# Cutting the last stage of a block kernel into pieces of 512, 384 and 128 tokens in place of 512, 256 and 256

## The chip, the core and the metric

The kernel runs on one core of a Trainium2 chip. The metric is the device time of one execution in microseconds; a comparison goes by the median of several runs.

## The reference

One layer of a streaming encoder, with 1024 tokens, 1024 channels (`D`) and a hidden width of 2816 (`DFF`): a mixing sub-layer, a gated feed-forward sub-layer, and a last root-mean-square norm. Only the end matters here:

```python
        a, bgate = jnp.split(jnp.einsum('bsd,df->bsf', h2, w_ffn_in[l]), 2, axis=-1)
        x = x + g2 * jnp.einsum('bsf,fd->bsd', jax.nn.silu(a) * bgate, w_ffn_out[l])

    return rms_norm(x, final_norm_g)
```

The final norm divides each token by the root of its mean square over all 1024 channels and multiplies each channel by a gain. So no output of a token can be scaled before all of its channels are there.

## The kernel before

Activations lie transposed: channels on the 128 partitions, tokens along the free axis. `x1[j]` for j from 0 to 7 is the residual of channel chunk j, 128 x 1024 in f32. Matrix products keep f32 precision by splitting every operand into a high and a low part in `fp32r`; one product of chunks is then three matmuls, high by high, high by low and low by high (`mm3`, L348, L349, L351), each with its own 128x128 weight load. Sums over partitions are matmuls with a matrix of ones in plain f32 (L1354), for which the profile shows two matmul rows each.

The feed-forward output product sums over 22 row chunks of the hidden tensor (`FC`). Eighteen of them are done by a scheme with seven products per 2x2 block in three groups; their results are added onto `x1`. The last four (`REST` = 18 to 21) are done plainly, and this is the stage that the change touches. Its tokens are cut into pieces (`PIECES`, L115), and the final norm of one piece is laid beside the products of the next:

- `piece_out(i, j)` (L1305): 12 matmuls for output chunk j of piece i into a PSUM tile `y`; VectorE evicts it by scaling it with the gate and adding `x1` (L1314); ScalarE squares the result (L1317). Where `on_pool(i, j)` is true, ScalarE then multiplies the chunk by its gain in place (L1321), since GpSimd is to do a plain product later.
- `piece_sum(i, j)` (L1324): VectorE adds the squares of chunk j to the sum.
- `piece_norm(i, parts)` (L1349): TensorE sums over partitions (`ss`); ScalarE takes the reciprocal root (L399, called through `rstd_start`) and half of its square (`rq`, L1356).
- `piece_rstd` (L1359): VectorE refines the root by one Newton step, `rft` (L1363) and `rf` (L1365). For the last piece `rf` lies in PSUM, for others in SBUF.
- `piece_scale(i, rf)` (L1328): chunk after chunk, GpSimd (L1342, by `rf` or for the last piece by an SBUF copy of it, `rp`, L1333) or VectorE (L1344, by gain and `rf` at once) scales, and SyncE issues the output DMA (L1347). With pieces narrower than 512 tokens, m = 512 / n chunks go into one tile and one DMA.

The loop at L1368 runs over pieces and, within one, over j. From the second piece on, after chunk 1 (`NORM_AT`) it emits the sum of the piece before, and after chunk 3 that piece's root and scales. For the last piece the root and the scales come behind everything, with the sum over four parts, the running sum of chunks 0 to 4 and the single squares of 5, 6 and 7 (`APART`). All chunks of the first two pieces are scaled on GpSimd, and of the last piece chunks 0, 3 and 5 (`POOL_LAST`), the others on VectorE.

Each engine works through its instructions in order, as the program emits them with `issue_after` hints; so do the DMA queues, among them SyncE's, which issues all outputs.

Of the kernel before, what the change touches and what calls it, by code (L numbers as in the profile page):

```python
# [38 lines left out]
ALU = mybir.AluOpType  # L39
# [5 lines left out]
KC = D // P  # L45
# [55 lines left out]
NORM_AT = 1  # L101
LAG = 2
APART = 3
POOL_LAST = (0, 3, 5)


PRODUCTS = "1265734"
# [4 lines left out]
REST = 2 * GROUP * GROUPS  # L112


PIECES = [(0, 512), (512, 256), (768, 256)]  # L115


FILL = 248
# [3 lines left out]
def block_kernel(ctx: ExitStack, tc: tile.TileContext, x0, xT, c, vecs, ada, w_first, w_plain, w_duals,  # L122
                 w_short, w_conf, w_o, w_fi, w_fo, w_last, outT):
    nc = tc.nc
# [27 lines left out]
    def ps_tile(name):  # L152
        return psp.tile([P, H], F32, tag="ps", name=name)

    def ps2_tile(name):
        return ps2p.tile([P, H], F32, tag="ps2", name=name)
# [1112 lines left out]
    n = 2 * GROUP * P  # L1269
# [26 lines left out]

    LAST = len(PIECES) - 1

    def wide_tile(name):
        return hl_tile(name, dt=F32)  # L1300

    def on_pool(i, j):
        return i < LAST or j in POOL_LAST

    def piece_out(i, j):  # L1305
        at, n = PIECES[i]
        h, off = at // H, at % H
        o = ps_tile("y")[:, :n]
        for f in range(REST, FC):
            xs = tuple(t[:, off : off + n] for t in hid[f, h])  # L1310
            c0 = (j % 4) * P
            mm3([o], slice(c0, c0 + P), ws[f, j // 4], [xs], f == REST, f == FC - 1)
        dst = x1[j][:, at : at + n]
        evac = nc.vector.scalar_tensor_tensor(out=dst, in0=o, scalar=modc(40 + j), in1=dst, op0=ALU.mult, op1=ALU.add)  # L1314
        piece_out.ins = evac.ins
        sq = wide_tile("sq")[:, :n]
        act = nc.scalar.activation(sq, dst, AF.Square, scale=1.0 / 32.0)  # L1317
        if i == LAST and j == KC - 1:
            load_rsqrt(act.ins)
        if on_pool(i, j):  # L1320
            nc.scalar.activation(dst, dst, AF.Copy, scale=ng[:, V_GFIN + j : V_GFIN + j + 1])  # L1321
        sqs.append(sq)

    def piece_sum(i, j):  # L1324
        with tc.issue_after(piece_out.ins):
            nc.vector.tensor_tensor(sqs[0], sqs[0], sqs[j], ALU.add)

    def piece_scale(i, rf):  # L1328
        at, n = PIECES[i]
        m = H // n  # L1330
        if i == LAST:
            rp = wide_tile("rp")[:, :n]
            nc.scalar.copy(rp, rf)  # L1333
        else:
            rp = rf
        for j in range(0, KC, m):
            ys = wide_tile("y") if m > 1 else x1[j][:, at : at + n]
            ys = ys.rearrange("p (m n) -> p m n", n=n)
            for d in range(m):
                y, src = ys[:, d], x1[j + d][:, at : at + n]  # L1340
                if on_pool(i, j + d):
                    nc.gpsimd.tensor_tensor(y, src, rp, ALU.mult)  # L1342
                else:
                    nc.vector.scalar_tensor_tensor(  # L1344
                        out=y, in0=src, scalar=ng[:, V_GFIN + j + d : V_GFIN + j + d + 1], in1=rf, op0=ALU.mult, op1=ALU.mult
                    )
            nc.sync.dma_start(outT[j : j + m, :, at : at + n].rearrange("m p n -> p m n"), ys)  # L1347

    def piece_norm(i, parts):  # L1349

        n = PIECES[i][1]
        ss, r, q = (t[:, :n] for t in (ps_tile("ss"), wide_tile("rf"), wide_tile("rq")))
        for part in parts:
            nc.tensor.matmul(ss, ones, part, start=part is parts[0], stop=part is parts[-1])  # L1354
        rstd_start(ss, eps1, "rf", n, lambda name: r)
        nc.scalar.activation(q, r, AF.Square, scale=0.5 ** 0.5)  # L1356
        return ss, r, q

    def piece_rstd(i, ss, r, q):  # L1359

        n = PIECES[i][1]
        t = ps2_tile("rft")[:, :n]
        nc.vector.scalar_tensor_tensor(out=t, in0=ss, scalar=EPS, in1=q, op0=ALU.add, op1=ALU.mult)  # L1363
        out = ps2_tile("rf")[:, :n] if i == LAST else r
        nc.vector.scalar_tensor_tensor(out=out, in0=t, scalar=1.5, in1=r, op0=ALU.subtract, op1=ALU.mult)  # L1365
        return out

    for i in range(len(PIECES)):  # L1368
        acc, sqs = sqs[0] if i else None, []
        lag = LAG if i == LAST else 0  # L1370
        for j in range(KC):
            piece_out(i, j)
            if j > lag and j - lag < KC - APART * (i == LAST):
                piece_sum(i, j - lag)
            if i and j == NORM_AT:
                norm = piece_norm(i - 1, [acc])
            if i and j == NORM_AT + 2:
                with tc.issue_after(piece_out.ins):
                    rf = piece_rstd(i - 1, *norm)
                piece_scale(i - 1, rf)  # L1380
    piece_scale(LAST, piece_rstd(LAST, *piece_norm(LAST, [sqs[0]] + sqs[KC - APART :])))


# [70 lines left out]
```

## Time and profile before

| | us |
|---|---|
| median of 3 runs | 1476.24 |
| their range | 1476.24 to 1478.43 |
| the profiled execution | 1477.93 |
| span of its instructions | 1476.2 |
| first piece, 512 tokens, from the first matmul | 1419.6 to 1441.2 |
| middle piece, 256 tokens | 1441.2 to 1453.6 |
| last piece, 256 tokens | 1453.6 to 1465.7 |
| from there to the end of the span | 10.5 |

PE is TensorE's matmuls, PEld its weight loads, DVE VectorE, ACT ScalarE, POOL GpSimd, SP SyncE. A row of a timeline gives the start from the beginning of the span, the duration (both in us), the engine, the line of the kernel, the operation, what it writes and reads, the shape and how many instructions are merged into the row; in brackets stands the idle time of the engine before it and what ended that. A row of a group gives count, busy time, mean duration in ns, and idle time before. Matmuls are pipelined: a matmul's duration includes its way through the array, and the pace is read from the distance of starts.

### The profile page before, as it was taken

Reading aid. Unit: us, or ns where it says so; the run is one execution under the profiler, and the core shown is the slowest. Engines: PE = TensorE matmul, PEld = TensorE weight load, DVE = VectorE, ACT = ScalarE, POOL = GpSimd, SP = SyncE. Lnnn points to the kernel's source line nnn. Section 1 sums busy time; section 2 is a strip of 40 time slices with the busy share of each in tenths; the row PEclk is TensorE's granted clock in tenths of the full one; section 3 lists DMA queues with packets and bytes.
Section 4 is the critical chain, followed back from the end, with each engine's and each line's share of the span. In section 5 each row is a group of like instructions: output and inputs, shape, how many; then the busy total and the mean of one; then the engine's idle time right before and its main releaser. Section 6 shows DMA issues by size and latency. Waiting matters only on the chain.

```text
span 1476.2 us, 17809 instructions
## 1 busy us (share of the span) xinstructions
PE 1462.0 (99%) x6475; PEld 1200.4 (81%) x6475; DVE 1177.7 (80%) x1623; ACT 617.0 (42%) x896; POOL 513.3 (35%) x459
## 2 busy tenths in 40 slices
PE   9999999999999999999999999999999999999997
PEld 5888888888888888878888878888888888888887
DVE  7999888887998969999687699777777765677755
ACT  4653433333333335555235465444444443222235
POOL 0036677767877771111022001101111015535005
PEclk9999999999999999999999999999999999999999
DMA  8522213222222267376685337655455449988403
GB/s 342 188 64 72 100 58 128 72 86 100 91 67 86 82 219 285 105 237 213 200 311 172 117 100 235 209 176 168 150 192 166 146 149 371 357 287 276 156 1 115
DMA packets 83274, 245.36 MB, mean 166 GB/s; under 512 B 9585, under 2 KB 11761, under 8 KB 83186
## 3 DMA queue, kind: packets, MB, share of 16 engines
q1 hardware_dynamic: 42352, 136.01, 27.6%
q0 software_dynamic: 36944, 95.44, 19.6%
q10 hardware_dynamic: 3890, 12.78, 2.3%
q8 instruction: 51, 0.84, 0.2%
q14 instruction: 37, 0.30, 0.1%
HBM read 181.79 MB, written 62.39 MB: 165 GB/s over the span
## 4 chain that ended last, share of the span: by engine, by line
PE 91%; DVE 6%; DMA 1%; issue 1%; ACT 1%; POOL 0%; POOLq 0%; DVEq 0%; ACTq 0%
PE bank L351 11%; PE bank L348 11%; PE bank L349 11%; PE x L351 7%; PE x L348 7%; PE x L349 7%; PE z L349 4%; PE z L348 4%; PE z L351 4%; PE y L349 3%; PE y L348 3%; PE y L351 3%; PE yb L351 2%; PE yb L348 2%; PE yb L349 2%; PE mix L349 2%
## 5 line engine op out<-in xcount | busy, mean ns | idle before, releaser
L220 ACT CAST wh<-raw 128x1024 fp32r<-128x1024 f32 (+2 forms) x254 | 256.3, 1011 | 485.2 <-PE bank L349 133.6
L221 POOL TENSOR_TENSOR wl<-raw,wh 128x1024 fp32r<-128x1024 f32 x84 | 204.5, 2444 | 81.8 <-ACT wh L220 81.8
L221 DVE TENSOR_TENSOR wl<-raw,wh 128x1024 fp32r<-128x1024 f32 (+2 forms) x170 | 195.0, 1147 | 47.5 <-ACT wh L220 46.2
L838 DVE SCALAR_TENSOR_TENSOR c<-diff,vec,c 128x512 f32<-128x512 f32 x232 | 171.0, 753 | 4.4
L1170 POOL DMA_DIRECT2D hid<-stage x71 | 37.8, 533 | 347.0 <-DVE stage L389 341.0
L348 PE MATMUL bank<-th,wh 128*128 128x512 f32 x288 | 112.0, 389 | 0.0
L349 PE MATMUL bank<-tl,wh 128*128 128x512 f32 x288 | 112.0, 389 | 0.0
L351 PE MATMUL bank<-th,wl 128*128 128x512 f32 x288 | 112.0, 389 | 0.0
L838 DVE SCALAR_TENSOR_TENSOR c<-u,wsum,c 128x512 f32<-128x512 f32 x112 | 84.3, 753 | 2.6
L240 POOL TENSOR_TENSOR raw<-raw 128x1024 f32<-128x1024 f32 x12 | 29.2, 2430 | 130.4 <-DVE wl L221 92.8
L388 ACT CAST stage<-g 128x512 fp32r<-128x512 f32 x62 | 38.4, 622 | 65.9 <-DMA hid<-stage 35.4
L351 PEld LDWEIGHTS bank<-th,wl 128*128 128x128 f32 x288 | 54.1, 188 | 11.3
L349 PEld LDWEIGHTS bank<-tl,wh 128*128 128x128 f32 x288 | 54.1, 188 | 11.2
L348 PEld LDWEIGHTS bank<-th,wh 128*128 128x128 f32 x288 | 54.1, 188 | 11.2
L389 DVE TENSOR_TENSOR stage<-g,stage 128x512 fp32r<-128x512 f32 x62 | 42.4, 689 | 25.3 <-ACT stage L388 25.3
L1196 POOL DMA_DIRECT2D th<-hid x71 | 38.0, 535 | 53.2 <-PE x L351 31.9
L348 PE MATMUL x<-th,wh 128*128 128x512 f32 x144 | 56.1, 390 | 0.0
L349 PE MATMUL x<-tl,wh 128*128 128x512 f32 x144 | 56.0, 389 | 0.0
L351 PE MATMUL x<-th,wl 128*128 128x512 f32 x144 | 56.0, 389 | 0.0
L348 PE MATMUL yb<-zsh,wh 128*128 128x512 f32 x128 | 49.8, 389 | 0.0
L349 PE MATMUL yb<-zsl,wh 128*128 128x512 f32 x128 | 49.8, 389 | 0.0
L351 PE MATMUL yb<-zsh,wl 128*128 128x512 f32 x128 | 49.8, 389 | 0.0
(798 smaller groups left out, 4211.3 us busy)
## 6 DMA issues: line engine op xcount, KB each, us to landing
hid<-stage POOLq DMA_DIRECT2D x71, 512.0 KB, 4.4
raw<-in_w_fi SPq DMA_DIRECT2D x51, 512.0 KB, 3.7
raw<-in_w_duals SPq DMA_DIRECT2D x48, 512.0 KB, 3.5
th<-hid POOLq DMA_DIRECT2D x71, 256.0 KB, 5.7
tl<-hid POOLq DMA_DIRECT2D x71, 256.0 KB, 5.7
ada<-in_ada SPq DMA_DIRECT2D x24, 512.0 KB, 5.9
raw<-in_ada SPq DMA_DIRECT2D x24, 512.0 KB, 4.6
raw<-in_w_fo SPq DMA_DIRECT2D x24, 384.0 KB, 5.7
```

The source lines that it names most:

```text
L220: hi = nc.scalar.copy(wh, raw)
L221: lo = lo_engine.tensor_tensor(wl, raw, f32(wh), ALU.subtract)
L240: eng.tensor_tensor(a["s1"], a["21"], a["22"], ALU.add)
L348: nc.tensor.matmul(ps, wh, xh, start=first, stop=False, skip_group_check=again)
L349: nc.tensor.matmul(ps, wh, xl, start=False, stop=False, skip_group_check=again)
L351: mm3.ins = nc.tensor.matmul(ps, wl, xh, start=False, stop=last, skip_group_check=again).ins
L388: t_split.act = nc.scalar.copy(hi, src).ins
L389: t_split.ins = nc.vector.tensor_tensor(lo, src, f32(hi), ALU.subtract).ins
L838: tap.ins = nc.vector.scalar_tensor_tensor(out=out, in0=src[:, s : s + H], scalar=wt, in1=acc, op0=ALU.mult, op1=ALU.add).ins
L1170: nc.gpsimd.dma_start(hid_dram[key], s)
L1196: nc.gpsimd.dma_start(t, hid_dram[key][:, s])
```

## The change

`PIECES` becomes 512, 384 and 128 tokens. `POOL_SCALES` tells for each piece which chunks GpSimd scales: all of the first, 0 to 4 of the middle one, and 0, 3 and 5 of the last as before. Chunks 5, 6 and 7 of the middle piece are scaled by VectorE, and they are emitted after the last chunk of the last piece, ahead of the last piece's own sum, root and scales; their output DMAs are issued there. ScalarE no longer multiplies these three chunks by their gain. The middle piece's root now lies in PSUM, so ScalarE makes an SBUF copy of it for GpSimd. With m = 512 // 384 = 1 the middle piece is scaled in place and has eight output DMAs of one chunk; the last has two DMAs of four chunks each (4 x 128 tokens).

In each engine's order the count of TensorE's instructions stays the same; VectorE gets four more, ScalarE two fewer and GpSimd three fewer, and SyncE issues 18 output DMAs in place of 16.

```diff
-POOL_LAST = (0, 3, 5)
+POOL_SCALES = (range(KC), range(5), (0, 3, 5))
...
-PIECES = [(0, 512), (512, 256), (768, 256)]
+PIECES = [(0, 512), (512, 384), (896, 128)]
...
     def on_pool(i, j):
-        return i < LAST or j in POOL_LAST
+        return j in POOL_SCALES[i]
...
-    def piece_scale(i, rf):
+    def piece_scale(i, rf, chunks=range(KC), rp=None):
+
         at, n = PIECES[i]
         m = H // n
-        if i == LAST:
+        if i and rp is None:
             rp = wide_tile("rp")[:, :n]
             nc.scalar.copy(rp, rf)
-        else:
-            rp = rf
-        for j in range(0, KC, m):
+        for j in chunks[::m]:
             ys = wide_tile("y") if m > 1 else x1[j][:, at : at + n]
...
                 if on_pool(i, j + d):
-                    nc.gpsimd.tensor_tensor(y, src, rp, ALU.mult)
+                    nc.gpsimd.tensor_tensor(y, src, rp if i else rf, ALU.mult)
...
-        out = ps2_tile("rf")[:, :n] if i == LAST else r
+        out = ps2_tile("rf")[:, :n] if i else r
...
-                piece_scale(i - 1, rf)
+                piece_scale(i - 1, rf, range(KC)[: len(POOL_SCALES[i - 1])])
+    with tc.issue_after(piece_out.ins):
+        piece_scale(LAST - 1, rf, range(len(POOL_SCALES[LAST - 1]), KC), ())
     piece_scale(LAST, piece_rstd(LAST, *piece_norm(LAST, [sqs[0]] + sqs[KC - APART :])))
```

## The prediction

> **What bounds the kernel now.** I read the page first (shares, then the chain), then the windows by stage, then each engine's timeline over the last 40 us.
>
> ```profile
> span 1476.2 us, 17809 instructions
> PE 1462.0 (99%) x6475; PEld 1200.4 (81%) x6475; DVE 1177.7 (80%) x1623; ACT 617.0 (42%) x896; POOL 513.3 (35%) x459
> 1419.60:1441.20 21.60, 21.60 (x97) 17.87 (x96) 10.16 (x14) 9.49 (x14) 0.00 (x0) 1.00 0.00 1
> 1441.20:1453.60 12.40, 12.40 (x100) 11.91 (x99) 8.66 (x16) 8.86 (x17) 3.02 (x3) 1.00 0.06 23
> 1453.60:1465.70 12.10, 12.10 (x101) 11.92 (x100) 8.42 (x17) 6.92 (x16) 10.84 (x10) 1.00 0.44 169
> 1465.70:1476.20 10.50, 1.88 (x10) 1.23 (x8) 3.40 (x8) 1.77 (x5) 5.12 (x8) 0.85 0.52 182
> ```
>
> The last four rows are the windows: length, then busy time of PE, PEld, DVE, ACT, POOL, granted clock, DMA share and GB/s. They are the three pieces and the tail. In the pieces PE is busy all the time at clock 1.00, so any extra TensorE time there moves the end. In the tail (10.5 us) TensorE only does the last sum, and a chain of small steps sets the end. The change touches both: it re-cuts the two later pieces and shortens the steps of the tail.
>
> **TensorE, the dear part.** Each piece is 8 output blocks of 12 products (4 row chunks of `hid`, 3 products each), 96 in all, whatever its width. Their pace is read from starts:
>
> ```profile
> 1424.88 0.39 PE L348 MATMUL y<-th,lwh 128*128 128x512 f32 x1
> 1441.20 0.28 PE L348 MATMUL y<-th,lwh 128*128 128x256 f32 x1
> 1443.96 0.28 PE L351 MATMUL y<-th,lwl 128*128 128x256 f32 x1
> 1456.32 0.28 PE L351 MATMUL y<-th,lwl 128*128 128x256 f32 x1
> 1456.53 0.30 PEld L1354 LDWEIGHTS ss<-sq,ones 128*128 128x128 f32 x2
> 1456.85 0.19 PEld L348 LDWEIGHTS y<-th,lwh 128*128 128x128 f32 x1
> 15.25 2.31 PEld L535 LDWEIGHTS clock<-rx0r,ones 128*128 128x128 f32 x20
> 1465.57 0.28 PE L351 MATMUL y<-th,lwl 128*128 128x256 f32 x1
> 1465.69 1.89 PE L1354 MATMUL ss<-sq,ones 128*128 128x256 f32 x8
> ```
>
> From 1424.88 to 1441.20 lie 72 products of 512 columns: 0.227 us each. From 1441.20 to 1443.96 lie 23 steps of 256: 0.120 us each. The straight line through both is 0.013 us plus 0.107 us per 256 columns; it gives 0.173 us for 384 columns and 0.067 us for 128.
>
> At 128 columns the line need not hold, because every product loads its own 128x128 weights. Two rows tell what a load takes. At 1456.53 TensorE is idle (the product before started at 1456.32 and was due for a successor at 1456.44): two loads span 0.30 us there and one lasts 0.19, so the second starts 0.11 us after the first, with nothing else in its way. In the 20 clock-keeping products of 128 columns at 15.25, loads follow each other every (2.31 - 0.19) / 19 = 0.112 us. No row shows loads of this size closer together than that. So I bound a 128-column product from below by 0.112 us, loads back to back. The upper end, while it stays one pass, is 0.123: plain products of 256 columns (the last row: four sums, two rows each, eight rows in 1.89 us, so 0.215 apart) have a fixed part of only 0.002 us over their streaming of 2 x 0.107, these products one of 0.013, and the 0.011 between them may come on top of the load. I take 0.120, the 256-column row, as the nearest: same instruction, same weights. Then the narrow piece costs as much as a 256-column one though it does half the work.
>
> Sum on TensorE: the middle piece goes from 96 x 0.120 to 96 x 0.173, +5.1 us; the last stays at 96 x 0.120, 0.0; the sum over squares of the middle piece is 384 wide in place of 256, 2 x 0.107 = +0.2. The last product of the kernel, at 1465.57 now, starts at T = 1470.9. That is the cost.
>
> **The tail, the gain.** The rows of the tail, with groups that give the slope by width:
>
> ```profile
> 1465.89 0.48 DVE L1314 SCALAR_TENSOR_TENSOR x<-y,mod,x 128x256 f32<-128x256 f32 x1 [0.48 <-PE y L351]
> 1466.41 0.42 ACT L1317 ACTIVATE sq<-x 128x256 f32<-128x256 f32 x1 [1.02 <-DVE x L1314]
> 1467.61 0.47 ACT L399 ACTIVATE rf<-ss,eps 128x256 f32<-128x256 f32 x1 [0.70 <-PE ss L1354]
> 1468.12 0.42 ACT L1356 ACTIVATE rq<-rf 128x256 f32<-128x256 f32 x1
> 1468.57 0.43 DVE L1363 SCALAR_TENSOR_TENSOR rft<-ss,rq 128x256 f32<-128x256 f32 x1 [2.20 <-ACT rq L1356]
> 1469.04 0.43 DVE L1365 SCALAR_TENSOR_TENSOR rf<-rft,rf 128x256 f32<-128x256 f32 x1
> 1469.50 0.37 ACT L1333 COPY rp<-rf 128x256 f32<-128x256 f32 x1 [0.97 <-DVE rf L1365]
> 1469.91 2.05 DVE L1344 SCALAR_TENSOR_TENSOR y<-x,ng,rf 128x256 f32<-128x256 f32 x5 [0.44 <-ACT rp L1333]
> 1469.95 2.09 POOL L1342 TENSOR_TENSOR y<-x,rp 128x256 f32<-128x256 f32 x3 [1.22 <-ACT rp L1333]
> L1314 DVE SCALAR_TENSOR_TENSOR x<-y,mod,x 128x256 f32<-128x256 f32 x16 | 7.6, 480 | 5.8 <-PE y L351 5.7
> L1314 DVE SCALAR_TENSOR_TENSOR x<-y,mod,x 128x512 f32<-128x512 f32 x7 | 5.3, 751 | 5.4 <-PE y L351 5.4
> L1317 ACT ACTIVATE sq<-x 128x256 f32<-128x256 f32 x16 | 6.6, 414 | 8.0 <-DVE x L1314 8.0
> L1317 ACT ACTIVATE sq<-x 128x512 f32<-128x512 f32 x7 | 4.4, 633 | 9.3 <-DVE x L1314 9.3
> ```
>
> DVE loses (751 - 480) / 2 = 0.135 us per 128 columns, ACT 0.11. Counted from T (now 1465.57), with the hand-over of 0.03 to 0.04 us that stands between the rows: eviction T+0.32 to 0.67 (0.345 long), square to 1.02, the two passes of the last summand at 0.112 in place of 0.215 (0.58 in place of 0.78 from the square's end to the next step), reciprocal root 1.60 to 1.96, its square to 2.31, then two DVE steps of 0.30 to 2.98, the copy `rp` to 3.27. Now that copy ends at T+4.30. Five DVE scales of 0.41 - 0.135 take 1.4, to T+4.7; three on POOL about 1.2 (below). Now both end at T+6.47. Gain so far: 1.8 us.
>
> What DVE is given in addition lies in there: three scales of 384 columns, 0.41 + 0.135 = 0.55 each, 1.65 us, are queued between the last eviction (T+0.67) and the first root step (needed at T+2.34). They fill the 2.20 us for which DVE now waits there, shrunk to 1.67. Cost nothing; if DVE is slower beside POOL, each 0.1 us per scale costs 0.3 us at the end, since the whole root chain and the five last scales are queued behind.
>
> Now POOL and SP's queue, past which the three scales are moved.
>
> ```profile
> 1450.58 10.79 POOL L1342 TENSOR_TENSOR x<-x,rf 128x512 f32<-128x512 f32 x8 [81.86 <-DVE rf L1365]
> 1462.63 6.10 POOL L1342 TENSOR_TENSOR y<-x,rf 128x256 f32<-128x256 f32 x8 [1.26 <-DVE rf L1365]
> 1460.13 0.48 DVE L1314 SCALAR_TENSOR_TENSOR x<-y,mod,x 128x256 f32<-128x256 f32 x1 [0.95 <-PE y L351]
> 1462.03 0.42 DVE L1365 SCALAR_TENSOR_TENSOR rf<-rft,rf 128x256 f32<-128x256 f32 x1
> 1464.27 8.73 SPq L1347 DMA_DIRECT2D outT<-y  x8
> 1470.70 2.30 SPq L1347 DMA_DIRECT2D outT<-y  x4
> GB/s 380 357 53 0 0 0 0 0 0 275 374 380 386 340 386 374 386 363 386 380 386 375 380 386 369 65 0 0 0 0 0 0 0 0 0 0 0 0 0 0
> ```
>
> POOL: 10.79 / 8 = 1.35 us for 512 columns, 6.10 / 8 = 0.76 for 256, so 1.06 for 384 and about 0.45 for 128. The root of the first piece waits for four blocks of the middle one, which are 4 x 12 x 0.053 = 2.6 us later, and for wider DVE steps between (0.3), so POOL starts at 1453.4 and ends the first piece at 1464.2 (now 1461.4). The middle piece's products start at 1441.2 as now and end at 1458.7 (96 x 0.173, and two rows of 512 plain columns for the first piece's sum, 2 x 0.43). Its root comes after four blocks of the last piece and its own sum: 1458.7 + 48 x 0.120 + 0.65 = 1465.1. From the fourth block's eviction to the end of `rf` the two DVE rows above stand 2.3 us apart, from start to end; with the hand-over 2.4, and 0.5 for `rp`: POOL starts its five scales at 1468.0 and ends at 1473.3. Its last three can start at T+3.3 = 1474.2: it is free by 0.9 us. Had it kept all eight, it would come 2.3 us late; that is what the move saves.
>
> DMA: the GB/s row covers 1470 to 1477 in slices of 0.175 us. The last piece's 1.05 MB flow at some 380 GB/s from 1471.6 (0.9 us after the issue at 1470.70) to 1474.5, and the span ends 1.7 us later. After, two chains reach for the end. By TensorE: the second half of the last piece is issued at T+4.7, flows from T+5.6 for 0.7 us, and the span ends at T+8.0 = 1478.9. By POOL and SP: the outputs of middle chunks 5 to 7 stand in SP's queue behind chunk 4, which POOL ends at 1473.3. From 1474.2 four chunks of 0.197 MB flow in 2.1 us, to 1476.3, and the last piece's 0.52 MB behind them in 1.4, to 1477.7; the span ends at 1479.4. The second is later. It holds 48 narrow products where the first holds 96: its end is 1473.65 + 48 c for c us per narrow product.
>
> **The sum.** 1479.4 is +3.2 us on the span: +5.3 on TensorE, and a tail of 8.5 us in place of 10.6. The profiled execution took 1477.93 us for its span of 1476.2, so 1.7 lie around it; the median of the runs is 1476.24, and put on that the forecast is 1479.4 us as well. With c = 0.112 it is +2.8, with 0.123 +3.4.
>
> **Rivals.** *The narrow products run on the line, 0.067 us: no change.* Then TensorE ends when it does now, T = 1465.8. For it: nothing but the line. Against it: the two load rows. The tail's gain would still not show, because POOL's chain ends last: 1473.65 + 48 x 0.067 = 1476.9, +0.6 us. The forecast's sign turns on this price: below c = 0.116 the end is within 3.0 us of now. The Trainium skill, "TensorE: Matmul & The Clock Gate", section "Back-to-back issue gap", gives about 81 ns for a sustained pair of weight load and 128-column matmul; by it, an estimate, the end would be 1473.65 + 48 x 0.081 = 1477.5, and this rival would hold. No row of this trace has loads that close.
>
> *The narrow products lose the single pass.* Plain 128-column products come every 0.112 us, and a plain sum needs two of them (eight rows for four sums above): 0.224 us per product, T later by 96 x 0.104 = 10.0 us, TensorE's chain the last: T+8.0 = 1488.9, slower by 0.9%. For it: no row shows this kind of product under 256 columns. Against it: the changed program's instruction order has one product where there was one, of the same kind.
>
> *DVE falls behind.* Sums of squares slow down beside POOL, which now runs through the whole last piece:
>
> ```profile
> 1445.24 0.43 DVE L1326 TENSOR_TENSOR sq<-sq 128x256 f32<-128x256 f32 x1 [0.48 <-ACT sq L1317]
> 1451.30 2.29 DVE L1326 TENSOR_TENSOR sq<-sq 128x256 f32<-128x256 f32 x2
> ```
>
> That is 1.15 us each for the two, against 0.43 before POOL starts. A block of the narrow piece has 1.44 us, eviction and sum then need 1.5: some tenths on top, for the last three scales of the middle piece too (end 1473.2 by the sum, 0.1 before POOL's), within the forecast's range.
>
> **How the numbers follow.** A measurement of this kernel tells about 0.2%, 3.0 us, from no change. The forecast's case (weight loads set the pace) gets 0.70; its own range is +2.0 to +4.5, so it lies on both sides of the bound: 0.42 slower by over 0.2%, 0.28 within. The line gets 0.12 (0.10 within, 0.02 faster, if tail steps are shorter than interpolated). The lost pass gets 0.18, all slower. Together slower 0.60, same 0.38, faster 0.02. The range takes in the first two cases, 1476.0 to 1482.0, and leaves out the third.
>
> **What would show it.** Right: narrow products about 0.12 us apart, the last one starting near 1471, about 8.5 us from there to the end, POOL idle just before its last three scales, DMA without a gap from chunk 4 on. Wrong: a pace near 0.07 (then POOL is busy without a gap to the end) or near 0.22; a root step on DVE that waits for the three scales and not for ACT.

## The result and the profile after

The changed kernel takes 1491.55 us (median of five, 1490.66 to 1492.97) against 1477.35 (1476.24 to 1480.24) for the kernel before on the same chip: slower, ratio 1.0094 with a 95% interval of 1.0081 to 1.0107, +14.2 us where +3.2 was forecast. The profiled execution took 1491.55 us with a span of 1489.7.

TensorE at the start of the stage, in the profile before and then after:

```profile
1419.44 0.39 PE L348 MATMUL y<-th,lwh 128*128 128x512 f32 x1
```

```profile
1422.11 0.39 PE L348 MATMUL y<-th,lwh 128*128 128x512 f32 x1
```

The stage begins 2.7 us later though all that precedes it is the same program. In the first 25 us the granted clock averaged 1.00 in the one profile and 0.93 in the other, but that average does not settle it: in the profiles of other runs below that have 0.93 there too, the stage begins anywhere from 1417.6 to 1423.5. Why the start shifts is not shown; executions of the kernel before scatter by some 4 us. So stages are compared from this row on: from here to the end of the span it is 56.7 us before and 67.6 after, +10.9.

The windows of the changed kernel (length, busy time of PE, PEld, DVE, ACT and POOL, granted clock, DMA share, GB/s):

```profile
1443.90:1461.40 17.50, 17.50 (x99) 17.02 (x98) 10.68 (x16) 10.28 (x17) 5.50 (x4) 1.00 0.12 43
1461.50:1467.90 6.40, 4.55 (x38) 4.14 (x36) 4.39 (x5) 2.07 (x7) 5.64 (x5) 1.00 0.43 166
1468.10:1480.80 12.70, 12.70 (x62) 12.70 (x61) 4.47 (x11) 3.01 (x9) 4.94 (x5) 0.50 0.27 97
1480.80:1489.70 8.90, 2.20 (x10) 1.91 (x9) 3.90 (x11) 1.34 (x5) 1.28 (x3) 0.50 0.37 125
```

The first row is the middle piece, 17.5 us as forecast. The second and third are the last piece: first 1.85 us in which TensorE is not busy, then 12.7 us at a granted clock of 0.50, to the end of the products. TensorE's timeline gives both, and the pace:

```profile
1463.71 0.27 PE L348 MATMUL y<-th,lwh 128*128 128x128 f32 x1
1463.82 0.28 PE L349 MATMUL y<-tl,lwh 128*128 128x128 f32 x1
1463.94 0.28 PE L351 MATMUL y<-th,lwl 128*128 128x128 f32 x1
1466.06 0.91 PE L1353 MATMUL ss<-sq,ones 128*128 128x384 f32 x2 [1.85 <-DVE sq L1326]
...
1480.35 0.41 PE L348 MATMUL y<-th,lwh 128*128 128x128 f32 x1
1480.56 0.41 PE L349 MATMUL y<-tl,lwh 128*128 128x128 f32 x1
1480.78 0.41 PE L351 MATMUL y<-th,lwl 128*128 128x128 f32 x1
```

Narrow products come every 0.11 us at first and every 0.21 at the end. Between them TensorE waits 1.85 us for VectorE's last sum of squares (L1326) before it can sum over partitions. Why that sum is late, VectorE's and GpSimd's timelines show:

```profile
1455.07 0.68 DVE L1364 SCALAR_TENSOR_TENSOR rf<-rft,rf 128x512 f32<-128x512 f32 x1
...
1460.35 0.61 DVE L1314 SCALAR_TENSOR_TENSOR x<-y,mod,x 128x384 f32<-128x384 f32 x1
1461.55 1.68 DVE L1326 TENSOR_TENSOR sq<-sq 128x384 f32<-128x384 f32 x1 [0.59 <-ACT sq L1317]
1463.15 0.61 DVE L1314 SCALAR_TENSOR_TENSOR x<-y,mod,x 128x384 f32<-128x384 f32 x1
1464.35 1.66 DVE L1326 TENSOR_TENSOR sq<-sq 128x384 f32<-128x384 f32 x1 [0.59 <-ACT sq L1317]
```

```profile
1455.90 11.24 POOL L1341 TENSOR_TENSOR x<-x,rf 128x512 f32<-128x512 f32 x8 [85.08 <-DVE rf L1364]
1473.20 4.94 POOL L1341 TENSOR_TENSOR x<-x,rp 128x384 f32<-128x384 f32 x5 [6.07 <-ACT rp L1334]
1484.79 1.28 POOL L1341 TENSOR_TENSOR y<-x,rp 128x128 f32<-128x128 f32 x3 [6.65 <-ACT rp L1334]
```

While GpSimd scales the first piece, from 1455.9 to 1467.1, a sum of 384 columns takes 1.7 us. Eviction, the wait for the square and the sum then take 2.8 us per block (1460.35 to 1463.15), where TensorE gives a block every 2.08 (12 x 0.173). VectorE falls behind by 0.7 us a block over the last blocks of the middle piece.

So two things were seen that the forecast's sum does not contain: a wait of TensorE and a fall of the granted clock. The experiments ask where the wait comes from, and whether the clock falls by the wait, by the thin products, or by both. Products are called thin here when they stream for about half of the time that their weight load takes.

### The profile page after: what moved, and what is told of

The parts are those of the page before. It is cut to its first block, busy times and chain, and to the rows that moved or that the text cites. A ratio compares the mean times of both kernels' runs of the same rounds, so it can differ in the third digit from the quotient of the medians.

```text
span 1489.7 us, 17805 instructions
## 1 busy us (share of the span) xinstructions
PE 1475.6 (99%) x6475; PEld 1212.6 (81%) x6475; DVE 1180.3 (79%) x1626; ACT 617.0 (41%) x894; POOL 512.4 (34%) x456
## 4 chain that ended last, share of the span: by engine, by line
PE 90%; DVE 7%; issue 1%; ACT 1%; DMA 1%; DVEq 0%; ACTq 0%
PE bank L351 11%; PE bank L349 11%; PE bank L348 11%; PE x L351 7%; PE x L349 7%; PE x L348 7%; PE z L348 4%; PE z L351 4%; PE z L349 4%; PE y L351 3%; PE y L349 3%; PE y L348 3%; PE yb L349 2%; PE yb L351 2%; PE yb L348 2%; PE mix L348 2%
## 5 line engine op out<-in xcount | busy, mean ns | idle before, releaser
L351 PEld LDWEIGHTS bank<-th,wl 128*128 128x128 f32 x288 | 54.1, 188 | 11.2
L349 PEld LDWEIGHTS bank<-tl,wh 128*128 128x128 f32 x288 | 54.1, 188 | 11.2
```

The lines of the kernel that those rows point to most:

```text
L349: nc.tensor.matmul(ps, wh, xl, start=False, stop=False, skip_group_check=again)
L351: mm3.ins = nc.tensor.matmul(ps, wl, xh, start=False, stop=last, skip_group_check=again).ins
```

## Experiments

**The sum and the root two blocks later** (the changed kernel otherwise): TensorE has other products to do before it needs VectorE's sum.

```diff
-            if i and j == NORM_AT:
+            if i and j == NORM_AT + 2 * (i == LAST):
...
-            if i and j == NORM_AT + 2:
+            if i and j == NORM_AT + 2 + 2 * (i == LAST):
```

> The changed kernel with the middle piece's sum over partitions and root emitted two blocks later in the last piece, so that TensorE need not wait 1.9 us for VectorE's sums. Two theories on why the granted clock falls to 0.5 some 6.6 us into the narrow piece. Thin products (each 128-column product streams for about 0.053 of the 0.111 us that its weight load takes, and that alone lets the clock down): no wait of TensorE, but the clock falls to 0.5 all the same and the pace goes from 0.111 to 0.213; about 1.9 us under the changed kernel, near 1489.5. Wait (the idle 1.9 us let the clock down): clock 1.00 and 0.111 us to the last product; 1.9 + 7 us under the changed kernel, near 1482.5.

Measured 1482.67 us (seven, 1481.24 to 1484.79; before: 1477.67), ratio 1.0035 (1.0023 to 1.0046). Its window over the whole last piece and its last products:

```profile
1461.10:1472.30 11.20, 11.20 (x99) 10.94 (x97) 7.90 (x16) 4.85 (x15) 5.88 (x6) 1.00 0.31 121
```

```profile
1472.16 0.28 PE L349 MATMUL y<-tl,lwh 128*128 128x128 f32 x1
1472.27 0.28 PE L351 MATMUL y<-th,lwl 128*128 128x128 f32 x1
```

No wait, clock 1.00, 0.11 us to the last product. Thin products alone do not let the clock down; the theory of the wait gave the time within 0.2 us. That closeness is partly luck: from the start of the stage the last product comes 8.2 us earlier than in the changed kernel (50.5 in place of 58.7 us), but the rest takes 10.7 us in place of 8.9, for GpSimd starts its scales of the middle piece only at 1472.1 and its last three directly behind them.

**Twice the work per weight load**: the last piece's products over 256 columns, of which 128 are used.

```diff
+        more = (256 - n) * (i == LAST)
-        o = ps_tile("y")[:, :n]
+        o = ps_tile("y")[:, : n + more]
...
-            xs = tuple(t[:, off : off + n] for t in hid[f, h])
+            xs = tuple(t[:, off - more : off + n] for t in hid[f, h])
...
-        evac = nc.vector.scalar_tensor_tensor(out=dst, in0=o, ...)
+        evac = nc.vector.scalar_tensor_tensor(out=dst, in0=o[:, more:], ...)
```

> The changed kernel with the last piece's products over 256 columns (768 to 1023), of which only the last 128 are evicted and used: twice the streaming per weight load, everything else the same, the 1.9 us wait of TensorE included. Thin products: clock stays at 1.00, pace 0.120; 72 products after the wait at 0.120 in place of 0.213, about 7 us under the changed kernel, near 1484.5 although TensorE does more. Wait: the clock falls to 0.5 as before and 256 columns then take 0.23 us: 1 to 2 us over the changed kernel, near 1493.

Measured 1483.52 us (seven, 1481.72 to 1485.04), ratio 1.0036 (1.0023 to 1.0049):

```profile
1463.61 0.59 PE L1354 MATMUL ss<-sq,ones 128*128 128x384 f32 x1 [1.64 <-DVE sq L1327]
```

```profile
1459.00:1472.90 13.90, 12.26 (x99) 11.80 (x97) 8.47 (x16) 5.20 (x15) 8.94 (x9) 1.00 0.31 118
```

The wait is there, 1.64 us, and the clock stays at 1.00. With twice the products' work the kernel is some 8 us faster than the changed one. This went as the theory of thin products said, the run above as the other. Neither is enough: this fall takes the wait and what surrounds it. The wait is 0.2 us shorter here than in the changed kernel; that this is not the reason, the stretches of the clock show below.

**The kernel before, with a wait put in**: VectorE instructions that leave the values as they are, ahead of the middle piece's last sum; three, two and one of them.

```diff
     def piece_sum(i, j):
+        for _ in range(HOLD * (i == 1 and j == KC - 1)):
+            nc.vector.scalar_tensor_tensor(out=sqs[j], in0=sqs[j], scalar=1.0, in1=sqs[j], op0=ALU.mult, op1=ALU.max)
```

> The kernel before, with three VectorE instructions (sq times 1, maximum with itself: the values stay) put ahead of the middle piece's last sum of squares, so that TensorE waits about 2.3 us at the same place, ahead of the middle piece's sum over partitions. Thin products: clock 1.00 to the end of the products, about +2.3 us, near 1479.5. Wait: the clock falls to 0.5 a few us later, some 60 products of 256 columns at 0.23 us in place of 0.12: +9 us, near 1486.

> The kernel before with two VectorE instructions (values stay) ahead of the middle piece's last sum: a wait of TensorE of about 2.5 to 3 us among 256-column products, longer than the 1.85 us of the changed kernel and shorter than the 4.1 us that halved the clock with three. If the wait's length alone decides, anything over about 1.8 us halves the clock for some 6.8 us: about +2.7 for the wait and +3.3 for the clock, near 1484. If thin products have their part in it, 256-column products around such a wait keep the clock at 1.00: near 1480.5.

> The kernel before with one VectorE instruction (values stay) in place of three put ahead of the middle piece's last sum, for a wait of TensorE of about 1.5 to 2 us among 256-column products. If a wait of that length lets the clock down by itself: clock 0.5 for one or two stretches of 3.41 us, 1.6 to 3.4 us on top of the wait, near 1482. If it takes thin products as well: clock 1.00, the wait alone, near 1479.3.

Measured 1483.65 us with three (ratio 1.0043, 1.0030 to 1.0057), 1482.35 with two (1.0031, 1.0022 to 1.0041), 1478.47 with one (1.0006, 0.9997 to 1.0015). TensorE's waits, in that order, came out at 4.13 us in place of 2.3, at 2.73 and at 1.33, since these instructions, too, took longer beside GpSimd:

```profile
1463.26 0.80 PE L1356 MATMUL ss<-sq,ones 128*128 128x256 f32 x1 [4.13 <-DVE sq L1328]
```

```profile
1457.50 0.48 PE L1356 MATMUL ss<-sq,ones 128*128 128x256 f32 x1 [2.73 <-DVE sq L1328]
```

```profile
1456.12 0.48 PE L1356 MATMUL ss<-sq,ones 128*128 128x256 f32 x1 [1.33 <-DVE sq L1328]
```

The windows with three, and with two:

```profile
1456.20:1461.10 4.90, 2.93 (x25) 2.73 (x23) 3.89 (x7) 2.79 (x6) 4.90 (x4) 1.00 0.44 169
1461.20:1467.90 6.70, 4.64 (x19) 4.46 (x20) 2.85 (x4) 1.60 (x4) 3.13 (x3) 0.50 0.37 145
1468.10:1474.50 6.40, 6.40 (x56) 6.40 (x55) 4.55 (x10) 2.69 (x6) 3.72 (x5) 1.00 0.13 43
```

```profile
1451.80:1458.20 6.40, 3.67 (x29) 3.42 (x29) 5.04 (x8) 3.11 (x7) 6.40 (x5) 1.00 0.46 175
1458.30:1461.60 3.30, 3.30 (x18) 3.30 (x17) 0.48 (x1) 1.24 (x3) 1.52 (x2) 0.50 0.53 205
1461.70:1468.10 6.40, 6.40 (x55) 6.40 (x55) 4.55 (x10) 2.69 (x6) 3.71 (x5) 1.00 0.12 42
```

Among 256-column products a wait of 2.73 or 4.13 us halves the clock too, but it comes back soon: after some 3.4 us with two, some 6.8 with three. That is read from one profile each; the mean clocks of the other executions with two, 0.996 to 0.999, leave open whether it fell in all of them. With three neither theory had the time (1479.5 and 1486). With one, 1.33 us, the clock stays at 1.00 over the whole piece. So thin products are not needed for the fall; a longer wait does it without them. What differs in the changed kernel is that the clock does not come back.

**Wide products late**: the changed kernel with its wait, and blocks 5, 6 and 7 of the last piece over 256 columns as above (`more` only for j > 4).

> The changed kernel, with 1.85 us of wait among thin products as it is, but with the products of blocks 5, 6 and 7 of the last piece over 256 columns (the last 128 used). Theory: thin products, once the clock is halved, keep it there, since they stream for half the time only; wide ones let it recover, as in the kernel with the 4.1 us wait, some 3.4 to 6.8 us after they begin. Then the clock falls near 7 us into the last piece as in the changed kernel and is back at 1.00 before the last product or at it, and the time is 0 to 2.5 us under the changed kernel, near 1490. Rival: once halved this late, the clock stays for 13 us or more whatever the products are: clock 0.5 to the end, and 36 products of 256 columns at 0.213 as before: no change, near 1491.5.

Measured 1488.18 us (four, 1487.15 to 1491.77; before: 1477.33), ratio 1.0074 (1.0055 to 1.0093). The windows, and the first wide products:

```profile
1462.80:1468.10 5.30, 3.46 (x28) 3.14 (x27) 4.39 (x5) 1.00 (x4) 5.30 (x5) 1.00 0.46 176
1468.20:1478.30 10.10, 10.10 (x49) 10.10 (x48) 2.75 (x7) 3.22 (x9) 2.94 (x4) 0.50 0.15 57
1478.50:1481.20 2.70, 2.70 (x25) 2.70 (x25) 1.88 (x4) 1.03 (x3) 2.14 (x3) 1.00 0.61 217
```

```profile
1475.77 0.52 PE L348 MATMUL y<-th,lwh 128*128 128x256 f32 x1
...
1478.43 0.28 PE L348 MATMUL y<-th,lwh 128*128 128x256 f32 x1
```

That is 10.9 us over the kernel before, where the changed kernel has 14.2: some 3 us less, and 0 to 2.5 were expected. The clock stays halved through all the thin products, 7.6 us, and is back 2.6 us after the first wide one. Thin products keep a halved clock down; that is shown. At half clock 256 columns take 0.21 us (1475.77 to 1478.43 hold 12 or 13 products), just as 128 do.

**Only the pieces, without VectorE's share**: the changed kernel with all eight chunks of the middle piece on GpSimd.

```diff
-POOL_SCALES = (range(KC), range(5), (0, 3, 5))
+POOL_SCALES = (range(KC), range(KC), (0, 3, 5))
```

> The changed kernel with all eight chunks of the middle piece left to GpSimd, as the kernel before has it; the pieces stay 512, 384 and 128. GpSimd was idle for 6.6 us ahead of its last three scales, so three more of 1.0 us should fit: within 0.5 us of the changed kernel by either theory on the clock, near 1491.5. If the move of three scales to VectorE had a cost of its own (1.65 us ahead of the root's two steps), this would be faster by up to 1.6 us.

Measured 1490.43 us (four, 1486.39 to 1491.27), ratio 1.0080 (1.0059 to 1.0100), not told apart from the changed kernel. One execution of the four took 1486.39 us with a mean granted clock of 0.997, the others 1490.08 to 1491.27 with 0.991 to 0.992; the one at 1486.39 us is the profiled one, and it has the same wait of 1.85 us. So with one and the same wait the clock need not fall; by the mean clocks it fell in the other three, and about 4 to 5 us hang on it here. Where it holds, GpSimd's eight scales set the end: its last three start at 1479.6, directly behind them, and from the last product to the end are 9.9 us.

**Only VectorE's share, without the pieces**: 512, 256 and 256, with chunks 6 and 7 of the middle one on VectorE at the end.

```diff
-PIECES = [(0, 512), (512, 384), (896, 128)]
+PIECES = [(0, 512), (512, 256), (768, 256)]
...
-POOL_SCALES = (range(KC), range(5), (0, 3, 5))
+POOL_SCALES = (range(KC), range(6), (0, 3, 5))
```

> One part of the change alone: pieces of 512, 256 and 256 as in the kernel before, but VectorE scales the middle piece's chunks 6 and 7 at the end (two in place of three, since two chunks share a DMA), and the middle root is copied for GpSimd. Two scales of 0.41 us fit into the 2.2 us in which VectorE waits for the last root: no change within 1 us, near 1477.5, by either theory.

Measured 1477.39 us (ten) against 1478.00, ratio 0.9995 (0.9985 to 1.0005): no change. The two scales take 0.86 us and VectorE still idles before the root:

```profile
1465.28 0.86 DVE L1343 SCALAR_TENSOR_TENSOR y<-x,ng,rf 128x256 f32<-128x256 f32 x2
1467.68 0.43 DVE L1362 SCALAR_TENSOR_TENSOR rft<-ss,rq 128x256 f32<-128x256 f32 x1 [1.54 <-ACT rq L1355]
```

**Sums with one operand in PSUM**: the changed kernel, with the middle piece's running sum kept there.

```diff
-        sq = wide_tile("sq")[:, :n]
+        sq = (ps_tile if i == 1 and j == 0 else wide_tile)("sq")[:, :n]
...
-            nc.vector.tensor_tensor(sqs[0], sqs[0], sqs[j], ALU.add)
+            out = sqs[0] if i != 1 else (wide_tile if j == KC - 1 else ps_tile)("acc")[:, : PIECES[i][1]]
+            nc.vector.tensor_tensor(out, sqs[0], sqs[j], ALU.add)
+            sqs[0] = out
```

> The changed kernel with the middle piece's running sum of squares kept in PSUM, so that VectorE's sums have one operand in SBUF and one in PSUM in place of two in SBUF; nothing else moves. Theory: TensorE's 1.85 us wait comes from sums of 1.7 us beside GpSimd (0.56 alone), which happens only with two SBUF operands. Then sums take about 0.56, the wait goes, the clock stays 1.00, the narrow pace is 0.111 to the end, and the forecast's own sum holds: about 3 us over the kernel before, near 1480.5. Rival: the sums are slow for another reason (the chain of eviction, square and sum): the wait and the drop of the clock stay, near 1491.

Measured 1480.49 us (ten, 1478.29 to 1483.11) against 1478.00, ratio 1.0019 (1.0010 to 1.0028). A sum of the middle piece, GpSimd beside it, and the window of the last piece:

```profile
1460.64 0.57 DVE L1327 TENSOR_TENSOR acc<-acc,sq 128x384 f32<-128x384 f32 x1 [0.59 <-ACT sq L1317]
1462.72 0.56 DVE L1327 TENSOR_TENSOR acc<-acc,sq 128x384 f32<-128x384 f32 x1 [0.59 <-ACT sq L1317]
```

```profile
1456.08 9.98 POOL L1343 TENSOR_TENSOR x<-x,rf 128x512 f32<-128x512 f32 x8 [85.86 <-DVE rf L1366]
```

```profile
1461.40:1472.50 11.10, 11.10 (x98) 10.84 (x97) 5.88 (x15) 5.39 (x14) 7.47 (x7) 1.00 0.36 137
```

The sums take 0.57 us in place of 1.7, also the last one, which writes to SBUF; the wait is gone, the clock holds, and GpSimd's eight scales take 10.0 us in place of 11.2. This is the change as the forecast had counted it, and it comes out at +2.5 us (forecast +2.8 at the lower bound of the narrow product's price, and 1480.5 for this run).

**Pieces of 512, 320 and 192**, sums in PSUM as above.

> Pieces of 512, 320 and 192 with the sums in PSUM. If the weight load sets the pace of narrow products, 192 columns go at 0.111 us as 128 do: the last product 1.7 us later than in the kernel before, the tail about 1 us shorter, about +0.8 us, near 1478.3. If the width set it (the line 0.013 + 0.107 per 256), 192 columns take 0.093 us: last product no later than before, near 1476.6.

Measured 1477.94 us (ten) against 1478.00, ratio 0.9995 (0.9983 to 1.0007): no change. The pace of 192 columns:

```profile
1465.48 0.27 PE L351 MATMUL y<-th,lwl 128*128 128x192 f32 x1
1465.59 0.28 PE L348 MATMUL y<-th,lwh 128*128 128x192 f32 x1
1465.71 0.27 PE L349 MATMUL y<-tl,lwh 128*128 128x192 f32 x1
1465.82 0.28 PE L351 MATMUL y<-th,lwl 128*128 128x192 f32 x1
```

0.11 us, as for 128 columns, where the line through the wider products gives 0.093: below 256 columns the weight load sets the pace. No version tried is faster than the kernel before.

## Why the prediction was wrong

The sign was right and the time was not: +14.2 us lies outside the range, which ended at 1482.0.

*The price of the narrow products* held. It was bounded from below by 0.112 us, taken as 0.120, and came out at 0.111; the taken value, the 256-column row, was too high by 0.009, and the weight-load rows were the better ones. For 384 columns 0.173 was forecast and measured. With sums in PSUM the last product starts 50.5 us after the start of the stage (1422.0 to 1472.5) where it was 46.1: +4.4, against +5.3 forecast with 0.120. The Trainium skill's 81 ns for such a pair ("TensorE: Matmul & The Clock Gate", "Back-to-back issue gap") does not hold for these products: 111 ns, at 192 columns too.

*The tail's steps* held. In the changed kernel the root steps on VectorE take 0.30 us each, the copy 0.27, the five scales 1.38, where 0.30, 0.27 and 1.4 were forecast. With sums in PSUM, from the last product's start (1472.52) to the end of the span (1480.8) are 8.3 us: 8.5 were forecast for the chain by GpSimd and SyncE, 8.0 for TensorE's own. The profile's chain that ended last is TensorE's, so the forecast had the wrong one of two chains last, which by its own sum lie 0.5 us apart.

*VectorE's three scales at no cost* held: giving them back to GpSimd does not gain, and VectorE alone with two of them does not lose. (The moved scales are three instructions more on VectorE by the profiles, 1626 in place of 1623, not the four named above.)

*"DVE falls behind"* is the step that failed. It was priced at some tenths, for the narrow piece alone, and from a row of 1.15 us for a 256-column sum. The chain that counts was in the middle piece, whose sums grow to 384 columns while GpSimd runs: eviction, square and sum take 2.8 us per block where TensorE takes 2.08. With what hangs behind it, TensorE's wait, it cost 1.85 us. The run with an operand in PSUM shows the cause: it changes nothing but where the sums lie, and the wait is gone. The Trainium skill says it in "GPSIMD Engine Reference", first table: GpSimd shares its SBUF interfaces with VectorE and contends with VectorE instructions that have two SBUF inputs. The traces agree: 1.7 us with two, 0.57 with one.

*The granted clock*, the dearer of the two, was not in the sum at all, and I took it as given: every window that I had quoted for the products showed 1.00, but none of them held narrow products or a wait of TensorE. By the profiles, from the start of the stage on, the changed kernel takes 67.6 us and the one without wait 58.8 (1422.0 to 1480.8): 8.8 us for the wait and what it triggers. 1.85 are the wait itself, the other 7 come with the halved clock: some 60 products at 0.213 in place of 0.111 are 6.1, the rest are the last sum's passes and what hung on them. By the medians against the kernel before it is 14.2 against 2.5, some 3 us more than in the two profiles, and these 3 us are not explained.

*The rival of the lost pass* had 1488.9 for the span, and 1489.7 was measured, by another mechanism. Its 0.224 us per product looks like the 0.213 that was seen, but the first 24 narrow products and all of them in the runs without the wait have 0.111. A time that fits does not confirm a mechanism; the pace row by row and the clock column do.

What lets the clock down can be read further from the traces. In each of them the granted clock changes only at points that lie 3.41 us or a multiple of it apart: it stands at 0.50 for 3.41, 6.83 or 10.24 us before it comes back, and at 1.00 for 13.65 us between two falls and for 1443.84 us, 423 times 3.413, ahead of the fall in the changed kernel. So TensorE's work can be counted from one such point to the next. Around the wait, each with the stretch that follows it, stand the changed kernel, the run with all chunks on GpSimd, and the one with twice the work per weight load:

```profile
1464.58:1467.99 3.41, 1.93 (x14) 1.67 (x14) 1.95 (x3) 1.62 (x5) 2.56 (x2) 1.00 0.40 154
1467.99:1471.40 3.41, 3.41 (x19) 3.41 (x18) 0.76 (x3) 0.62 (x3) 0.00 (x0) 0.50 0.20 77
```

```profile
1464.78:1468.20 3.42, 2.15 (x15) 1.88 (x16) 1.74 (x3) 2.02 (x6) 2.35 (x2) 1.00 0.45 176
1468.20:1471.61 3.41, 3.41 (x33) 3.41 (x33) 2.29 (x7) 1.40 (x5) 0.00 (x0) 1.00 0.14 54
```

```profile
1460.72:1464.13 3.41, 1.77 (x14) 1.44 (x12) 2.76 (x5) 0.81 (x2) 3.41 (x3) 1.00 0.43 167
1464.13:1467.55 3.42, 3.42 (x29) 3.29 (x28) 0.47 (x2) 1.94 (x6) 0.56 (x1) 1.00 0.36 140
```

The first two have the same wait of 1.85 us. In the changed kernel 1.48 of it lie in one stretch, and the clock falls at its end; in the other run a point of change cuts it into 0.58 and 1.27, and the clock holds. So it counts where the wait lies between these points. The third has all of its 1.64 us in one stretch, more than the first, and less busy time, and the clock holds: thin products help to bring the fall about. Each is one profile, but the mean clocks of the other executions agree: 0.990 to 0.992 in all five of the changed kernel, 0.997 to 0.999 in all seven with twice the work. Among 256-column products it fell when a stretch had 2.04 or 2.68 us of the waits (4.13 and 2.73 us in all). Still open is what exactly is counted within a stretch, and with what bound. The Trainium skill, "TensorE: Matmul & The Clock Gate", Part 1, describes a gate that judges the array's activity in free-running windows of 3.4 us. The traces agree with it in the length of the stretches, and in that the same wait falls differently into them from one execution to another.

## What to carry to other kernels

Price a narrow product by its weight load, not by its width, and look at what the narrow stream does to the clock: here thin products ran at full clock, but once a wait of 1.85 us had halved it, they kept it halved until wide ones came. An engine that only accumulates beside the main chain needs its own sum per block, evict, wait and add, against the pace of TensorE, with the contention that it will have where the change moves it. A VectorE sum of two SBUF tiles beside GpSimd can take three times as long; keeping one operand in PSUM avoids it.

## What the runs showed of the hardware that I had not expected

- The granted clock fell to 0.50 after a wait of 1.85 us and stayed there for 12.7 us of continuous 128-column products; in the run with wide products late it came back 2.6 us after 256-column products began.
- It changes only at points 3.41 us or a multiple of it apart, and the same wait of 1.85 us halves it or not by how much of it lies between two of them (1.48 us did, 1.27 did not).
- At half clock 128 and 256 columns both take 0.21 us, at full clock 0.111 and 0.120: doubling the columns costs next to nothing, and here it gained some 8 us.
- A VectorE add of 384 columns takes 1.7 us beside GpSimd with two SBUF operands and 0.57 with one in PSUM, and GpSimd's own eight scales go from 11.2 to 10.0 us.
